# A hybrid decoder layer: the input projection of the last 1024 tokens as a stage of its own, in Strassen's seven products

## The chip, the cores and the metric

One Trainium2 chip, one NeuronCore. The metric is the device time of one execution in microseconds (us), the median of several runs; a profile gives one execution instruction by instruction. PE is TensorE's matmul, PEld its weight load, DVE is VectorE, ACT is ScalarE, POOL is GpSimd, SP is the queue that issues every DMA of this kernel.

## The reference, cut to what matters

One decoder layer is run for a prompt of 2048 tokens and for 8 sample tokens that share its weights. Each token is a row of 1024 numbers.

```python
h = rmsnorm(x, g_mix_pre)
proj = h @ w_in                       # 1024 x 4608
u_ssm, u_pool, q_mem, gates = proj[:512], proj[512:1024], proj[1024:1536], proj[1536:]   # by columns
o_ssm  = s5_branch(u_ssm)             # complex scan over time, gelu, then y * sigmoid(y @ w_glu + b)
o_pool = pool_branch(u_pool)          # trailing means over 2, 4, 8, 16 tokens, 128x128 map, scale
o_mem  = mem_attention(q_mem)         # 4 heads over 256 memory tokens
merged = sum_b sigmoid(gates_b) * (o_b @ w_branch_up[b])      # b = ssm, pool, mem
x = x + rmsnorm(merged @ w_out, g_mix_post)
x = x + rmsnorm(swiglu(rmsnorm(x, g_ffn_pre)), g_ffn_post)
```

The s5 scan and the pooling windows run along time, so a quarter of the tokens needs what the quarter before it left (`carry`, `hist`). All arithmetic is float32. A matmul of float32 quality is made of three matmuls of a faster type: both operands are split into a high and a low part (`split`: ACT copies the high part, DVE or POOL subtracts), and hi·hi, hi·lo and lo·hi are added up in PSUM.

## The kernel before

The prompt is worked on in four quarters of 512 tokens (`NQ`, `TQ`); quarter 1 carries the 8 samples too. Channels lie on the 128 partitions, tokens along the free dimension. A *block* below is one tile of 128 output channels from 1024 input channels for one quarter: 8 slices of the input, 3 matmuls each, 24 matmuls of 512 columns (`mmk`). Every weight tile is loaded (512 KB), split on ACT and DVE (on POOL for the kinds in `ON_POOL`) and used; a fixed list `_SEQ` says in which order, and `prefetch` keeps `AHEAD` = 3 of them under way.

The mixing stage (pool `mix`) does one quarter after the other:

- `ssm_project`: 4 blocks with tokens on the partitions; its result is turned by transposes in `s5_group`.
- `projections`: 4 blocks for the queries (`q_project`), 4 for the pool branch (`pool_project`), and woven among them the attention: `scores`, `transposed`, `attend`, and `pool_mix`.
- `gates`: for each of three branches 8 pairs of a gate block (`gt`, 24 matmuls) and a branch-up block (`ub`, 12 matmuls, input 512 channels); the sigmoid of the first times the second is added to `acc`. Before the branch that needs it, `glu` runs on the s5 output.
- `out_project`: 8 blocks; `residual` then needs the row norm of all of them, adds x and writes the new x to DRAM.

What isn't on the main chain of matmuls (s5 of the quarter, norms, residual of the quarter before) is written as generators in `background`, and `step` takes one piece of it between blocks; `flush` takes all that is left. A scheduler then orders the instructions of each engine by place in the program; `tc.high_priority(offset=n)` moves a piece up by n places. The main matmuls keep their order (`Tensor`).

The feed-forward input (`ffn_in`, pool `half`) already works in Strassen's form, on two quarters at once: `sums` writes the seven left operands to DRAM (`d_S`), `left` reads them back through the 4 buffers `xr` and splits them into 56 tiles `S`, `w_pair` makes the seven right operands from two weight tiles, and `product` runs each as 24 matmuls of half a quarter's width: 4 slices, 3 matmuls, 2 halves. So two blocks for two quarters take 168 matmuls of 256 (or 258) columns. `LEAD` = 700 moves the first `left` forward. A tile of a new pool waits for the tile whose memory it takes (`reuse_waits="tile"`). The last stage (pool `down`) is the feed-forward output.

At the change from mixing to feed-forward, `residual` of quarter 3 isn't in the background: it is run to its end (`run(res)`). It loads x through `xr` (`load_x`), and in program order these loads stand ahead of those of `left`.

Of the kernel before, what the change touches and what calls it, by code (L numbers as in the profile page):

```python
# [19 lines left out]
P = 128  # L20
# [14 lines left out]
SB = ((0, 1), (2, 3))  # L35
KH = KD // 2
# [9 lines left out]
AHEAD = 3  # L46
STEPS = ((1, 1, 1), (2, 1, 1), (1, 1, 1), (1, 1, 1))
# [9 lines left out]
def _weight_plan():  # L57
# [16 lines left out]
    for q in range(NQ):  # L74
# [5 lines left out]
        seq += wo + us if q + 1 < NQ else wo  # L80
    for sb in range(len(SB)):
        seq += [("f1", f) for f in range(NF)]
# [3 lines left out]
    return seq  # L86


_SEQ = _weight_plan()
_STORED = [k for k in dict.fromkeys(_SEQ) if k[0] not in ("KT", "V", "f1")]  # L90
_STORED += [(k, f) for f in range(NF) for k in ("fa", "fb")]
# [37 lines left out]
def trunk(ctx, tc, nc, I, O):  # L129
# [5 lines left out]
    BUFS = {"U": 5, "G": 2, "ops": 6, "h": 16, "br": 24, "acc": 8, "rb2": 1,  # L135
            "xr": 4, "tmp": 7, "rb": 1, "wr": 4, "wh": 4, "wl": 4, "wt": 2,
            "ev": 4, "S": 56, "f": 52, "z": 8}
    SIZE = {"tmp": 528, "ops": 512, "G": 512, "wr": 1024, "wh": 1024, "wl": 1024, "wt": 1024,
            "ev": HW_, "S": HW_, "f": HW_, "z": HW_}
    COMMON = ("xr", "tmp", "rb", "rb2", "wr", "wh", "wl")  # L140
# [6 lines left out]
    def slot(tag, dt=F32):  # L147
        n = nm(tag)
        p = base if tag in COMMON else stage[0]
        return p.tile([P, SIZE.get(tag, W520)], dt, tag=tag, name=n, bufs=BUFS[tag])  # L150

# [35 lines left out]
    mix = tc.tile_pool(name="mix", bufs=1, reuse_waits="tile")  # L187
    stage[0] = mix.__enter__()
    for tag in ("U", "G", "ops", "h", "br", "acc"):
        slot(tag)  # L190
    cv = small([P, 2, NB], "cv")
    pscale, bglu = cv[:, 0, :], cv[:, 1, :]
    ptab = small([P, NB, 4, 4], "ptab")
    hist = small([P, NB, 4, 4], "hist")
    V.memset(hist, 0.0)
    carry = [small([P, 16], "carry_re"), small([P, 16], "carry_im")]
# [11 lines left out]
    d_S = dram([len(SB), 7, KH, P, HW_], "d_S")  # L208
    d_f = dram([NQ, NF, P, HW_], "d_f")
# [42 lines left out]
    seq = _SEQ  # L252
    half = [None]
    wstate = {"emit": 0, "cur": 0, "buf": {}}
# [6 lines left out]
    def w_pair(f):  # L261
        wa, wb = w_load(("fa", f)), w_load(("fb", f))
# [14 lines left out]
    def w_emit(i):  # L277
        key = seq[i]
        if key[0] == "f1":
            wstate["buf"][i] = w_pair(key[1])  # L280
            return
# [15 lines left out]
    def prefetch():  # L297
        i = wstate["cur"]
        while wstate["emit"] < len(seq):
            pair = seq[wstate["emit"]][0] == "f1"  # L300
            if wstate["emit"] > i + (1 if pair else AHEAD) or pair and stage[0] is not half[0]:
                break
            w_emit(wstate["emit"])
            wstate["emit"] += 1
# [74 lines left out]
    def load_x(q, k, sl=None):  # L379
        t = slot("xr")  # L380
# [160 lines left out]
    r4 = small([P, 16], "r4")  # L541
# [235 lines left out]
    def s5_group(q, g, U, us, out):  # L777
# [6 lines left out]
        pu = psum2()  # L784
        for i in range(4):
            T.transpose(pu[:, i * P:(i + 1) * P], U[:, i * P:(i + 1) * P], ident)
        Ut = slot("U")
        S.activation(Ut[:, :512], pu, AF.Copy)
# [11 lines left out]
        Gr, Gi = slot("G"), slot("G")  # L800
# [47 lines left out]
        yT = slot("U")  # L848
        S.activation(yT[:, :TQ], pt, AF.Copy)
        if q == QS:  # L850
            V.tensor_copy(yT[:, TQ:W520], ysT)
# [3 lines left out]
    def s5(q, U, us, out):  # L855
        for g in range(4):
            yield from s5_group(q, g, U[g], us, out)

# [83 lines left out]
    def pool_project(q, m, h):  # L942
        n = width(q)
        w = wget("up", m)
        ps = pst(q)
        mmk(q, ps, w, h)
        pbt = slot("tmp")
        pb = pbt[:, :528].rearrange("p (s c) -> p s c", s=4)
        for p_, (o, nn) in zip(ps, blocks(q)):
# [53 lines left out]
    def q_project(q, m, h, qs):  # L1003
# [9 lines left out]
        if q == QS:  # L1013
            V.tensor_copy(qs[:, m, :], ps[-1][:, 256:264])
        return hi, lo
# [195 lines left out]

    def out_project(q, mg, z, st):
# [16 lines left out]
    def residual(q, z, st):  # L1229
# [5 lines left out]
        for k in range(KD):  # L1235
            xt = load_x(q, k)
# [10 lines left out]
        if q + 1 < NQ:  # L1247
            yield from second_scale(q)
# [21 lines left out]
    def sums(sb):  # L1270
        n = fwidth(SB[sb][0])
        rbs = [slot("rb"), slot("rb2")]
        for i, q in enumerate(SB[sb]):
            load_half(rbs[i], d_rb2, q)
        for k in range(KH):
            A = {}
            for i, q in enumerate(SB[sb]):
                for j in range(2):
                    t = slot("xr")
                    load_half(t, d_x2[:, k + j * KH], q)  # L1280
                    V.scalar_tensor_tensor(t[:, :n], t[:, :n], g_fpre[:, k + j * KH:k + j * KH + 1],
# [9 lines left out]
            for i, t in enumerate((A[0, 0], A[0, 1], s4, A[1, 1], s1, s2, s3)):  # L1291
                nc.sync.dma_start(d_S[sb, i, k, :, :n], t)
            yield

    PRODUCTS = (0, 1, 5, 4, 6, 3, 2)

    def left(sb):
        n = fwidth(SB[sb][0])
        got = {}
        for i in PRODUCTS:  # L1300
            for k in range(KH):
                raw = slot("xr")
                nc.sync.dma_start(raw[:, :n], d_S[sb, i, k, :, :n])
# [4 lines left out]

    def ffn_in(sb, got):
        n = fwidth(SB[sb][0])  # L1310
        w = n // 2
        for f_ in range(NF):
            B11, B21, T2, T1, T3, t4, B22 = wget("f1", f_)
            X, Z, Y = ([psum() for _ in range(2)] for _ in range(3))
            p1, u2, u3 = (slot("ev") for _ in range(3))
            f0, f1 = slot("tmp"), slot("tmp")

            def product(bank, i, wt, start):
                hi, lo = wt
                for u in range(2):  # L1320
                    us = slice(u * w, (u + 1) * w)
                    o = bank[u][:, :w]
                    for k in range(KH):
                        sl = slice(k * P, (k + 1) * P)
                        ah, al = got[i, k]
                        T.matmul(o, lhsT=hi[:, sl], rhs=ah[:, us], start=start and k == 0, stop=False,
                                 skip_group_check=not start)
                        T.matmul(o, lhsT=hi[:, sl], rhs=al[:, us], start=False, stop=False,
                                 skip_group_check=not start)
                        T.matmul(o, lhsT=lo[:, sl], rhs=ah[:, us], start=False, stop=k == KH - 1,  # L1330
                                 skip_group_check=not start)

            def both(fn):
                with tc.high_priority(offset=URGENT):
                    for u in range(2):
                        fn(u, slice(u * w, (u + 1) * w))

            def take(dst):
                both(lambda u, s: S.activation(dst[:, s], X[u][:, :w], AF.Copy))  # L1339

            def plus(dst, bank):
                both(lambda u, s: V.tensor_tensor(dst[:, s], dst[:, s], bank[u][:, :w], ADD))

            product(X, 0, B11, True)
            take(p1)
            product(Z, 1, B21, True)
            plus(p1, Z)
            step()
            product(X, 5, T2, False)
            take(u2)  # L1350
            product(Y, 4, T1, True)
            step()
            product(X, 6, T3, False)
            take(u3)
            plus(u3, Y)
            product(X, 3, t4, False)

            def f1_(u, s):
                S.activation(f1[:, s], X[u][:, :w], AF.Sigmoid)
# [274 lines left out]
```

## Time and profile before

| | |
|---|---|
| time, median of 3 runs | 3143.11 us (3140.39 to 3144.47) |
| the profiled execution: time / span | 3146.45 / 3144.5 us |
| mean granted TensorE clock | 0.975 |
| busy PE / DVE / ACT / POOL | 2996.9 / 1858.3 / 1214.7 / 741.6 us |
| quarters 2 and 3 of the mixing | about 915 to 1673 us |
| feed-forward input, output | about 1697 to 2598, 2602 to 3144 us |

The span is the time from the first to the last instruction; the time has a little more around it. "Busy" adds up an engine's instructions; a matmul's recorded duration overlaps that of the next, so PE is paced by when groups of a known number of matmuls end, not by its mean. A clock of 1.00 is 2.4 GHz, 0.5 is 1.2 GHz.

### The profile page before, as it was taken

What the parts mean: (1) busy time and instruction counts of PE and PEld (TensorE: products, weight loads), DVE (VectorE), ACT (ScalarE), POOL (GpSimd) and SP (SyncE); (2) the same over time, 40 slices, a digit from 0 to 9 for tenths busy, and PEclk for the clock granted to TensorE, in tenths of its full rate; (3) what the DMA queues carried; (4) which work ended last, traced back from release to release, by engine and by line L of the source; (5) the groups of instructions that cost most, each with busy time, mean ns of one, the idle gap of its engine ahead of it and who ended that gap; (6) DMA issues with size and microseconds to landing.
All of it is one profiled execution on the core that took longest, in us unless ns stands there. A gap on an engine that the chain in (4) does not pass through costs nothing.

```text
span 3144.5 us, 51655 instructions
## 1 busy us (share of the span) xinstructions
PE 2996.9 (95%) x20479; PEld 2764.9 (88%) x20479; DVE 1858.3 (59%) x3187; ACT 1214.7 (39%) x2105; POOL 741.6 (24%) x630
## 2 busy tenths in 40 slices
PE   7989998799999999999996999999999999999997
PEld 6778877689997888878885999999999998999997
DVE  7777756664538644585566855557555554445364
ACT  4532434322445333452333433335333334334343
POOL 2565244532245122440222000000000000011012
PEclk8989999899999999999997999999999999999999
DMA  6344333662334433354364732225222225445475
GB/s 210 112 161 138 120 121 116 163 218 91 127 121 149 137 102 127 120 174 133 110 219 143 233 114 76 78 77 175 81 81 81 81 84 176 153 153 170 159 253 171
DMA packets 205730, 433.02 MB, mean 138 GB/s; under 512 B 47472, under 2 KB 55216, under 8 KB 205488
## 3 DMA queue, kind: packets, MB, share of 16 engines
q1 hardware_dynamic: 205488, 429.72, 43.1%
q8 instruction: 160, 2.62, 0.4%
q14 instruction: 82, 0.67, 0.1%
HBM read 362.82 MB, written 66.49 MB: 137 GB/s over the span
## 4 chain that ended last, share of the span: by engine, by line
PE 82%; DVE 5%; DMA 5%; issue 3%; POOL 2%; ACT 2%; SPq 1%; DVEq 0%; POOLq 0%; ACTq 0%
PE pa L117 78%; PE pb L117 3%; DMA xr<-d_f 1%; DVE wl L172 1%; PE pb L120 1%; DMA xr<-in_ck 1%; DMA xr<-d_S 1%; DVE acc L1238 1%; DMA xr<-in_cv_t 0%; ACT wh L171 0%; SPq L679 0%; DMA ops<-d_ops 0%; POOL acc L1239 0%; DMA xr<-d_qs 0%; DVE G L815 0%
## 5 line engine op out<-in xcount | busy, mean ns | idle before, releaser
L117 PE MATMUL pa<-S,wh 128*128 128x258 f32 (+1 forms) x4928 | 887.4, 283 | 26.1 <-ACT S L171 20.1
L171 ACT ACTIVATE wh<-wr 128x1024 fp32r<-128x1024 f32 (+1 forms) x460 | 458.2, 996 | 1022.4 <-PE pa L117 744.1
L117 PEld LDWEIGHTS pa<-S,wh 128*128 128x128 f32 x4928 | 762.5, 190 | 29.4 <-ACT S L171 21.4
L117 PE MATMUL pa<-S,wl 128*128 128x258 f32 (+1 forms) x2464 | 693.6, 282 | 0.3 <-DVE wl L172 0.3
L117 PE MATMUL pa<-h,wh 128*128 128x512 f32 (+2 forms) x2560 | 667.2, 356 | 19.5 <-ACT tmp L1037 7.4
L172 DVE TENSOR_TENSOR wl<-wr,wh 128x1024 fp32r<-128x1024 f32 x372 | 434.2, 1169 | 393.5 <-ACT wh L171 380.8
L117 PEld LDWEIGHTS pa<-h,wh 128*128 128x128 f32 x2560 | 438.4, 192 | 86.5 <-ACT tmp L1037 7.6
L117 PE MATMUL pa<-br,wh 128*128 128x512 f32 (+2 forms) x1848 | 471.3, 351 | 15.0 <-ACT wh L171 8.8
L117 PE MATMUL pa<-f,wh 128*128 128x258 f32 (+1 forms) x2816 | 468.9, 283 | 5.9 <-DVE f L172 3.0
L117 PEld LDWEIGHTS pa<-S,wl 128*128 128x128 f32 x2464 | 465.6, 189 | 0.5 <-DVE wl L172 0.5
L117 PE MATMUL pa<-h,wl 128*128 128x512 f32 (+2 forms) x1280 | 420.7, 355 | 0.0
L117 PEld LDWEIGHTS pa<-f,wh 128*128 128x128 f32 x2816 | 400.1, 190 | 8.4 <-DVE f L172 4.3
L117 PEld LDWEIGHTS pa<-br,wh 128*128 128x128 f32 x1848 | 311.6, 190 | 62.8 <-ACT wh L171 8.8
L172 POOL TENSOR_TENSOR wl<-wr,wh 128x1024 fp32r<-128x1024 f32 (+1 forms) x88 | 214.2, 2436 | 442.2 <-ACT wh L171 392.5
L117 PE MATMUL pa<-f,wl 128*128 128x258 f32 (+1 forms) x1408 | 312.3, 283 | 4.5 <-DVE wl L172 4.5
L117 PE MATMUL pa<-br,wl 128*128 128x512 f32 (+2 forms) x924 | 295.4, 350 | 1.0 <-DVE wl L172 1.0
L117 PEld LDWEIGHTS pa<-h,wl 128*128 128x128 f32 x1280 | 231.4, 192 | 33.6
L1365 POOL TENSOR_TENSOR tmp<-tmp,ev 128x516 f32<-128x516 f32 (+1 forms) x44 | 59.9, 1362 | 841.2 <-ACT tmp L1364 820.9
L172 DVE TENSOR_TENSOR wl<-wt,wh 128x1024 fp32r<-128x1024 f32 x88 | 108.1, 1228 | 223.5 <-ACT wh L171 223.5
L117 PEld LDWEIGHTS pa<-f,wl 128*128 128x128 f32 x1408 | 229.8, 189 | 4.7 <-DVE wl L172 4.7
L117 PEld LDWEIGHTS pa<-br,wl 128*128 128x128 f32 x924 | 164.1, 190 | 24.3 <-DVE wl L172 1.4
L1339 ACT ACTIVATE ev<-pa 128x258 f32<-128x258 f32 (+1 forms) x264 | 101.0, 385 | 196.7 <-PE pa L117 166.8
(329 smaller groups left out, 3486.7 us busy)
## 6 DMA issues: line engine op xcount, KB each, us to landing
wr<-in_w_all SPq DMA_DIRECT2D x408, 512.0 KB, 3.5
ops<-d_ops SPq DMA_DIRECT2D x112, 256.0 KB, 3.6
xr<-in_x_t SPq DMA_DIRECT2D x80, 256.0 KB, 3.7
xr<-d_x SPq DMA_DIRECT2D x72, 256.0 KB, 4.1
wr<-in_w_all SPq DMA_DIRECT2D x40, 384.0 KB, 3.4
d_f<-tmp SPq DMA_DIRECT2D x44, 258.0 KB, 4.7
xr<-d_f SPq DMA_DIRECT2D x44, 258.0 KB, 3.7
d_f<-tmp SPq DMA_DIRECT2D x44, 256.0 KB, 4.3
```

What stands on the lines that cost most here:

```text
L117: self._done(self.nc.tensor.matmul(*a, **k))
L120: self._done(self.nc.tensor.transpose(*a, **k))
L171: S.activation(dst_hi, src, AF.Copy)
L172: (eng or V).tensor_tensor(dst_lo, src, f(dst_hi), SUB)
L1238: V.tensor_tensor(zk, zk, rb[:, :n], MUL)
L1339: both(lambda u, s: S.activation(dst[:, s], X[u][:, :w], AF.Copy))
L1365: G.tensor_tensor(f0[:, :n], f0[:, :n], p1[:, :n], MUL)
```

## The change

Quarters 0 and 1 stay as they are, except that the norm statistics of quarters 1 to 3 are all taken in quarter 0, and that quarter 1 has `sums_mix(1)` in its background: it writes the seven left operands of the normed x of quarters 2 and 3 to `d_h`. After quarter 1 three stages follow, each with its own pool:

- `ahead`: all 36 blocks of the input projection of quarters 2 and 3 as 18 pairs in seven products (`in_spilled`, on `seven`, which is the old body of `ffn_in`). Results, gates after their sigmoid, go to `d_p` in DRAM. In the background: s5 of quarter 2 (`s5_spilled`, its input read from `d_p`, its output written to `d_y`) and the `sums` of the first two quarters for the feed-forward.
- `late`: for quarters 2 and 3 the rest of the mixing (`mix_spilled`): `glu`, then 3 x 8 branch-up blocks whose gates are read back; during the first 8 of them (`beside`) the attention and the pool branch, from read-back projections. s5 of quarter 3 is the background of quarter 2, the residual of quarter 2 that of quarter 3. `PACE` says how many pieces per block.
- `half` and `down` as before; `f` has 50 tiles instead of 52.

The residuals of quarters 1 and 3, which end a pool, load x through `U`, not `xr`.

```diff
+MQ = (0, 1)
+PAIRS = [(("uc", 0), ("uc", 1)), (("uc", 2), ("uc", 3)), (("uq", 0), ("uq", 1)), (("uq", 2), ("uq", 3)),
+         (("up", 3), ("up", 2)), (("up", 1), ("up", 0))]
+PAIRS += [(("gt", b, j), ("gt", b, j + 1)) for b in (0, 1, 2) for j in range(0, 8, 2)]
+PACE = (1, 2, 2)
...
+    seq += [("seven", *p) for p in PAIRS]
+    for q in SB[1]:
+        seq += glu + ub(0)[:2] + [("pw",)] + ub(0)[2:] + ub(1) + ub(2) + wo
...
-    def s5_group(q, g, U, us, out):
+    def s5_group(q, g, U, us, out, tag="U", gtag="G"):
...
+        if U is None:
+            src = d_p[q % 2, SPILL["uc", g]].rearrange("(i h c) (s n) -> h s c i n", i=4, h=2, s=4)
+            for h in range(2):
+                for s in range(4):
+                    rows = slice(64 * h + 16 * s, 64 * h + 16 * s + 16)
+                    nc.sync.dma_start(Ut[rows, :512].rearrange("p (i n) -> p i n", i=4), src[h, s])
+        else:
+            pu = psum2()
+            for i in range(4):
+                T.transpose(pu[:, i * P:(i + 1) * P], U[:, i * P:(i + 1) * P], ident)
+            S.activation(Ut[:, :512], pu, AF.Copy)
...
+    def mix_spilled(q):
+        yT = []
+        for g in range(4):
+            t = slot("U")
+            nc.sync.dma_start(t[:, :TQ], d_y[q % 2, g])
+            yT.append(t)
+        KV = []
+        for src in (d_kt, d_v):
+            raw, hi, lo = slot("wr"), slot("kv", F32R), slot("kv", F32R)
+            nc.sync.dma_start(raw, src)
+            split(hi, lo, raw, G)
+            KV.append((hi, lo))
+        br = [glu(q, yT), [None] * NB, [None] * NH]
+        if q + 1 < NQ:
+            background.append(s5_spilled(q + 1, "U", "G"))
...
+        def beside(j):
+            if j < NH:
+                qt[j] = q_load(q, j)
+                pd[3 - j] = pool_project(q, 3 - j, None)
+            if 0 <= j - 1 < NH:
+                es[j - 1] = scores(q, j - 1, qt[j - 1], KV[0])
+            if 0 <= j - 2 < NH:
+                pT[j - 2] = transposed(q, j - 2, es[j - 2])
+            if 0 <= j - 4 < NH:
+                br[2][j - 4] = attend(q, j - 4, pT[j - 4], KV[1])
+                br[1][7 - j] = pool_mix(q, 7 - j, pd[7 - j], pw)
+        for b in range(3):
+            for j in range(KD):
...
+                gt = slot("gt")
+                nc.sync.dma_start(gt, d_p[q % 2, SPILL["gt", b, j]])
+                pu = psum()
+                mmk(q, [pu], wub, br[b], off=(j % 2) * NB * P)
...
+                with tc.high_priority(offset=URGENT):
+                    V.tensor_tensor(t, gt, pu, MUL)
+                if b == 0:
+                    with T:
+                        beside(j)
+                else:
+                    (V if b == 2 else G).tensor_tensor(acc[j][:, :TQ], acc[j][:, :TQ], t, ADD)
+                if b == 2:
+                    hi, lo = slot("br", F32R), slot("br", F32R)
+                    split(hi[:, :TQ], lo[:, :TQ], acc[j][:, :TQ])
+                    out.append((hi, lo))
+                step(PACE[b])
+        flush()
...
-            xt = load_x(q, k)
+            xt = load_x(q, k, tag="U" if q in (MQ[-1], NQ - 1) else "xr")
...
+    def in_spilled(got, *then):
+        for ka, kb in PAIRS:
+            out = slot("tmp")
+            fn = AF.Sigmoid if ka[0] == "gt" else AF.Copy
+            def corner(s, x):
+                S.activation(out[:, s], x, fn)
+            def end(c11, c12, c22):
+                for t, i, key in ((c11, 0, ka), (out, 1, ka), (c22, 1, kb), (c12, 0, kb)):
+                    if t is not out and fn != AF.Copy:
+                        S.activation(t[:, :TQ], t[:, :TQ], fn)
+                    nc.sync.dma_start(d_p[i, SPILL[key]], t[:, :TQ])
+            seven((ka, kb), got, TQ, corner, end)
+            if kb == ("uc", 3):
+                background.extend(then)
...
+    run(res)
+    mix.__exit__(None, None, None)
+
+    ahead = enter("ahead", {"wr": 3, "wt": 2, "ev": 3, "ops": 4, "S": 56}, {"ev": TQ, "S": TQ})
+    with tc.high_priority(offset=LEAD):
+        prefetch()
+        got = left(d_h, TQ)
+    background.append(second_scale(1))
+    in_spilled(got, s5_spilled(2, "xr", "xr"), sums_ffn(0))
+    flush()
+    ahead.__exit__(None, None, None)
+
+    late = enter("late", {"wr": 4, "U": 5, "G": 2, "ops": 6, "gt": 6, "kv": 4, "br": 24, "acc": 8})
+    for q in SB[1]:
+        mg = mix_spilled(q)
...
     run(res)
-    mix.__exit__(None, None, None)
...
+    late.__exit__(None, None, None)
+    half = enter("half", {"wr": 4, "wt": 2, "ev": 4, "S": 56}, {"ev": HW_, "S": HW_})
```

## Rows read from the trace of the kernel before

**Rows 1.** The page: busy time by engine; the chain that ended last, by engine

```profile
PE 2996.9 (95%) x20479; PEld 2764.9 (88%) x20479; DVE 1858.3 (59%) x3187; ACT 1214.7 (39%) x2105; POOL 741.6 (24%) x630
...
PE 82%; DVE 5%; DMA 5%; issue 3%; POOL 2%; ACT 2%; SPq 1%; DVEq 0%; POOLq 0%; ACTq 0%
```

**Rows 2.** Stretches: length; PE, PEld, DVE, ACT, POOL busy; clock; DMA share; GB/s

```profile
100.00:200.00 100.00, 85.63 (x406) 70.01 (x405) 82.96 (x219) 46.22 (x90) 64.59 (x119) 0.92 0.40 131
...
934.00:1026.00 92.00, 84.54 (x421) 68.24 (x420) 69.56 (x129) 47.09 (x107) 48.15 (x39) 0.98 0.44 147
...
1673.00:1697.00 24.00, 3.93 (x18) 3.61 (x18) 18.96 (x29) 7.74 (x13) 13.33 (x8) 0.54 0.48 149
1697.00:1744.00 47.00, 37.35 (x249) 34.92 (x248) 38.89 (x72) 26.20 (x47) 1.67 (x1) 0.84 0.74 230
...
1744.00:2161.00 417.00, 417.00 (x3487) 417.00 (x3488) 254.13 (x421) 158.68 (x283) 29.78 (x21) 1.00 0.39 115
```

**Rows 3.** Timeline of ACT: evictions of `out_project` (L1223) and of `ssm_project` (L770)

```profile
934.53 2.89 ACT L770 ACTIVATE U<-pa 128x128 f32<-128x128 f32 x16 [2.37 <-PE pa L117]
...
1282.85 0.58 ACT L1223 ACTIVATE tmp<-pa 128x512 f32<-128x512 f32 x1
...
1293.97 0.58 ACT L1223 ACTIVATE tmp<-pa 128x512 f32<-128x512 f32 x1
...
1313.38 2.87 ACT L770 ACTIVATE U<-pa 128x128 f32<-128x128 f32 x16 [2.38 <-PE pa L117]
```

**Rows 4.** Timeline of ACT in `ffn_in`: the same eviction of two successive tiles

```profile
2561.42 0.39 ACT L1339 ACTIVATE ev<-pa 128x256 f32<-128x256 f32 x1 [0.85 <-PE pa L117]
...
2581.31 0.39 ACT L1339 ACTIVATE ev<-pa 128x256 f32<-128x256 f32 x1 [0.85 <-PE pa L117]
```

**Rows 5.** Chain of waits, one piece of s5: 16 small matmuls

```profile
1048.85 1.78 PE pb L117 x16
```

**Rows 6.** Timelines of ACT, DVE, POOL, SP where mixing gives way to feed-forward

```profile
1672.88 0.60 ACT L1223 ACTIVATE tmp<-pa 128x512 f32<-128x512 f32 x1 [4.38 <-PE pa L117]
...
1681.16 11.31 DVE L1238 TENSOR_TENSOR acc<-acc,rb 128x512 f32<-128x512 f32 x8 [2.27 <-ACT rb L372]
...
1681.93 13.33 POOL L1239 TENSOR_TENSOR acc<-acc,xr 128x512 f32<-128x512 f32 x8 [27.90 <-DVE acc L1238]
...
1690.28 0.33 SPq L1303 DMA_DIRECT2D xr<-d_S  x1
...
1695.83 1.14 ACT L171 ACTIVATE S<-xr 128x516 fp32r<-128x516 f32 x2
```

**Rows 7.** The page: DMA issues, KB each, median us from issue to landing

```profile
d_f<-tmp SPq DMA_DIRECT2D x44, 256.0 KB, 4.3
xr<-d_f SPq DMA_DIRECT2D x44, 256.0 KB, 4.2
```

**Rows 8.** Groups of POOL, 934 to 1313 us: busy us, mean ns

```profile
L172 POOL TENSOR_TENSOR wl<-wr,wh 128x1024 fp32r<-128x1024 f32 x21 | 51.8, 2466 | 96.6 <-ACT wh L171 96.6
...
L172 POOL TENSOR_TENSOR br<-U,br 128x512 fp32r<-128x512 f32 x4 | 5.7, 1429 | 68.9 <-ACT br L171 68.8
```

**Rows 9.** Groups of DVE, 934 to 1313 us: busy us, mean ns

```profile
L172 DVE TENSOR_TENSOR wl<-wr,wh 128x1024 fp32r<-128x1024 f32 x40 | 50.5, 1262 | 54.1 <-ACT wh L171 49.9 <-PE pb L117 3.8
L1226 DVE TENSOR_TENSOR tmp<-tmp,tmp 128x512 f32<-128x512 f32 x7 | 18.0, 2571 | 10.2 <-ACT tmp L1223 10.2
L814 DVE TENSOR_TENSOR_SCAN G<-r,carry_re,G 128x128 f32<-128x128 f32 x16 | 12.4, 832 | 1.4 <-POOL G L807 1.4
...
L1238 DVE TENSOR_TENSOR acc<-acc,rb 128x520 f32<-128x520 f32 x8 | 10.6, 1378 | 0.6 <-ACT rb L372 0.6
...
L815 DVE TENSOR_TENSOR_SCAN G<-r,carry_im,G 128x128 f32<-128x128 f32 x16 | 6.4, 459 | 0.0
...
L820 DVE TENSOR_TENSOR tmp<-G,ops 128x512 f32<-128x512 f32 x4 | 2.7, 684 | 0.1
```

More of the change, by code (lines that the diff above doesn't have):

```diff
@@ L85, in _weight_plan @@
     seq += fo
[L86 to L91, printed above, removed]
+    ends.append(len(seq))
+    return seq, ends
+_SEQ, _ENDS = _weight_plan()
+_STORED = []
+for _k in _SEQ:
+    _STORED += [x for x in (_k[1:] if _k[0] == "seven" else [_k]) if x[0] not in ("KT", "V") and x not in _STORED]
 _WIDX = {k: i for i, k in enumerate(_STORED)}
@@ L150, in slot, with enter, keep @@
         return p.tile([P, SIZE.get(tag, W520)], dt, tag=tag, name=n, bufs=BUFS[tag])
+    def enter(name, bufs, sizes=()):
+        for tag in list(BUFS):
+            if tag not in COMMON:
+                del BUFS[tag]
+        BUFS.update(bufs)
+        SIZE.update(sizes)
+        guard = tc.tile_pool(name=name, bufs=1, reuse_waits="tile")
+        stage[0] = guard.__enter__()
+        for tag in bufs:
+            slot(tag)
+        wstate["end"] = ends.pop(0)
+        return guard
+    def keep(shape, tag):
+        return base.tile(shape, F32, tag=tag, name=nm(tag), bufs=1)
     def small(shape, tag, bufs=1, dt=F32):
@@ L298, in prefetch @@
         i = wstate["cur"]
-        while wstate["emit"] < len(seq):
-            pair = seq[wstate["emit"]][0] == "f1"
-            if wstate["emit"] > i + (1 if pair else AHEAD) or pair and stage[0] is not half[0]:
+        while wstate["emit"] < wstate["end"]:
+            if wstate["emit"] > i + (1 if seq[wstate["emit"]][0] == "seven" else AHEAD):
                 break
@@ L1371, in load_f @@
+            seven((("fa", f_), ("fb", f_)), got, n, corner, end)
     def load_f(q, n):
@@ L1472, in trunk @@
     background.append(s5_first(U, yT))
-    for q in range(NQ):
+    for q in MQ:
         br = [None] * 3
@@ L1480, in trunk @@
                 br[0] = glu(q, yT)
-                background.append(norm_stats(q + 1) if q + 1 < NQ else sums(0))
+                if q == 0:
+                    background.extend(norm_stats(j) for j in range(1, NQ))
+                else:
+                    background.append(sums_mix(1))
             if b == 2 and q == QS:
@@ L1512, in trunk @@
             prefetch()
-            got = left(sb)
+            got = left(d_S[sb], fwidth(SB[sb][0]))
         if sb + 1 < len(SB):
             background.append(second_scale(NQ - 1))
-            background.append(sums(sb + 1))
+            background.append(sums_ffn(sb + 1))
         ffn_in(sb, got)
         flush()
-    second.__exit__(None, None, None)
-    down = tc.tile_pool(name="down", bufs=1, reuse_waits="tile")
-    stage[0] = down.__enter__()
-    slot("z")
+    half.__exit__(None, None, None)
+    down = enter("down", {"wr": 4, "z": 8, "f": 50})
     for q in range(NQ):
```

251 lines of the change are left out of this document (146 added, 105 removed).

## The prediction

> **What bounds the kernel now.** I read the page first: PE is busy 95% of the span, and 82% of the chain that ended last is PE [rows 1]. So a saving of matmul time counts in full where PE is back to back, and the question is where it isn't. The view of stretches shows where: PE is full in the feed-forward input, idle 7.5 of 92 us while a quarter's projections and attention run, and far from full for 71 us where mixing gives way to feed-forward [rows 2]. Then I read the pace of PE off evictions that wait for it: two `out_project` blocks end 11.12 us apart, so a block of 24 matmuls of 512 columns takes 5.56 us, 0.2315 us each; `ssm_project`'s four blocks take 1313.38 - 1293.97 = 19.4 us; and one `ffn_in` tile of 168 matmuls of 256 columns takes 2581.31 - 2561.42 = 19.9 us, 0.1184 each [rows 3, 4]. Half the columns cost 0.511 of the time, so halving the width gives away little of the eighth that seven products save.
>
> **The saving on PE.** Removed for two quarters: 2 x (19.4 + 32 x 5.56) = 394.6 us. Added: 18 pairs x 19.9 = 358.2 us. Also removed are 32 transposes of the s5 input, at 1.78/16 = 0.11 us each [rows 5]: 3.5 us. Together -39.9 us. This half is well founded: the new stage is the same code as the stage that rows 4 are from. Everything below is about what the cut costs.
>
> **Hand-over 1, quarter 1 to `ahead`.** Before, `ssm_project` of quarter 2 followed at once and the residual of quarter 1 hid in the background. Now that residual is run to its end, as quarter 3's is today. What that does today: the last block ends at 1672.9, the norm chain takes 8.3 us, then eight steps of DVE and POOL 1.67 us apart, and the first `left` load is issued only at 1690.3, because the residual's x loads hold the `xr` buffers; the first split of an S tile is at 1695.8, and in the 71 us to 1744 PE gets through 249 feed-forward matmuls of 0.12 us plus small ones, about 31 us [rows 2, 6]. So today's hand-over costs 40 us, part of it at the low clock (0.54 and 0.84). The new one is better placed: x comes through `U`, so `left` may load and split during `out_project`, into memory that `h` has left. Of the right operands, t34 lies where two `U` buffers lay, so it waits for the residual, 8 to 24 us after the last block; the four products before it (96 matmuls, 11.4 us) don't. The last S tiles take the memory of `acc`, which is free when the last new x is in DRAM: 8 + 13 + about 2 + 4.3 us [rows 6, 7], then a load (4.2) and a split: some 33 us, when an unhindered first pair would be over at 19.9. The first pair then ends near 36: I take +17 us; bounds 10 and the 40 of today.
>
> **`ahead` itself.** DVE is busy 254 of 417 us in today's stage with PE full [rows 2]. Per 19.9 us pair it keeps four differences, the low halves and six additions, and loses the four swiglu products; it gains s5 of quarter 2 (57 us, below). That is some 75%, spread in 48 pieces. PE has no other cover to lose here: +2 us, bounds 0 and 10. The extra DMA (1 MB written per 20 us, and DMA share 0.39 there now) hides.
>
> **Hand-over 2, `ahead` to `late`.** `glu` needs four `yT` in `U`; two of these lie where the last pair's `ev` tiles lie. These must be added up, go through a sigmoid, be stored (4.3 us) and only then can `yT` be loaded (4.2 us) and split, the low half on POOL (1.43 us) [rows 7, 8]. Nothing else stands on PE's main chain. About 1.5 + 4.3 + 4.2 + 2 = 12 us; bounds 8 (what is on POOL goes early) and 20 (POOL does the four K/V and GLU splits of 2.47 us first).
>
> **The mixing that is left.** Here cover is gone. A branch-up block had a gate block of 5.56 us beside it; now its 12 matmuls (2.78 us) stand alone, while DVE keeps almost all its work. Per quarter PE has 48 + 288 + 36 matmuls of 512 (86 us), 48 of 256 (5.7), 48 transposes and small ones (7): 99 us up to `out_project`; in quarter 2 also s5 of quarter 3, 160 matmuls of 0.11: 117 us. DVE in quarter 2: 12 low halves at 1.26, 84 operations of 512 columns at 0.69 (GLU 8, queries 4, pool 8, attention 20, pool map 4, gate products 24, sums and splits of the third branch 16), 5 of small ones: 78 us; s5: 32 scans (18.8 us), 48 operations at 0.68, 6 of others: 57 us [rows 9]. 135 us of DVE against 117 of PE: DVE becomes the bound of quarter 2's mixing. At 100% busy that costs 18 us; at the 83% that DVE reached in the start, where it is the bound today [rows 2], 163 - 117 = 46. I take 27, nearer the lower end, since the start is one serial set-up and here four groups and a main chain interleave, and some query and pool work can run in hand-over 2. Quarter 3 has no s5, but the residual of quarter 2 (11.3 us as in rows 6, plus 8) falls into its first 8 blocks: DVE there 45 + 19 = 64 against PE's 55: +12 with friction. Then 2 x 2 us because the first branch-up block now waits for `glu`'s last split. Together 43. What goes away: a quarter today takes 1313.38 - 934.53 = 378.9 us for 19.4 + 177.9 + 564 x 0.2315 + 5.7 + about 31 of small matmuls = 364.6 us [rows 3], so 14 us per quarter, 28 for two, are lost in the stretches removed. Net +15 us; bounds -5 (18 + 5 - 28) and +45 (46 + 23 + 4 - 28).
>
> **Hand-over 3, `late` to feed-forward.** Today's 40 us. Now `left` needn't wait for `xr`; but both `wt` buffers lie under `U`, which the residual holds until about 22 us. Two products (5.7 us) run at once, then PE waits to about 25, starts at the low clock, and finishes the tile after 14 to 18 us: 25 + 16 - 20 = 21. Gain -18 us; bounds -25 and 0 (nothing gained).
>
> **Hidden.** `sums_mix(1)` in quarter 1's last gates: the same work (`sums`) runs in quarter 3's last gates today. The two norms more in quarter 0 lie under its last gates. The 6 fewer `f` tiles still leave room ahead. s5's 8 small loads per group stand on SP among loads that have their time. 0, bounds 0 and 4.
>
> **The sum.** -39.9 + 17 + 2 + 12 + 15 - 18 = -11.9 us against the profiled execution's own 3146.45: 3134.5. That execution is 3.3 us above the median of the runs shown, so 3131 us.
>
> **A rule against it.** `L1226` takes 2571 ns in the stretch where POOL makes the low halves of `wo` (2466 ns each), although an addition of that size takes 684 [rows 8, 9]; `L1238`, alternating with POOL, takes 1378. So VectorE and GpSimd hold each other up here. The Trainium skill, "SBUF — State Buffer", "Who interferes with whom", says why: the pair of ports that both share is locked for a whole instruction, and a VectorE operation with two SBUF inputs stands still while a GpSimd operation reads SBUF. By that rule, the trace agrees, the late mixing is the worst place for it, since POOL's work there (GLU and K/V splits, pooling sums, attention scaling) isn't made less.
>
> **The rivals.**
> - *VectorE with POOL in its way bounds the late mixing (slower).* Price: the excess seen in one quarter today, 7 x 1.9 + 8 x 0.7 + 16 x 0.37 = 25 us [rows 9], half of it beside `out_project` where DVE is idle. The scans' 6 are counted already; if the other 19 all fall into quarter 2's mixing and a third of them into quarter 3's, the late loss is 27 + 19 + 12 + 6 + 4 = 68, net +40: -39.9 + 17 + 2 + 12 + 40 - 18 = +13, 3156 us. It decides from a net late loss of 27 us on. For it: 135 against 117. Against: POOL is busy only 48 of 92 us in today's densest stretch. Chance 0.18.
> - *Every hand-over costs what today's costs (slower).* If `left` isn't early, hand-over 1 costs 40, hand-over 3 gains nothing: -39.9 + 40 + 2 + 14 + 15 + 0 = +31, 3174 us. For it: the order is a scheduler's. Against: `xr` is what held `left`, and it is free now. Chance 0.09.
> - *It evens out.* Hand-over 1 at 24 and late +20: -39.9 + 24 + 2 + 12 + 20 - 18 = 0, 3143 us. Chance 0.18.
> - *The cuts hide better than I think.* 10, 0, 8, -5, -25 with the saving: -52, 3091 us; half-way 3110. Chance 0.13.
> - That the seven products don't save: their pace would have to miss 21.9 us per pair; rows 4 say 19.9. Under 0.02, inside the others.
>
> **The numbers.** Forecast 3131 us, chance 0.42, own range 3112 to 3137. 0.2% is 6.3 us, about what a measurement of this kernel can tell from no change. Faster: 0.42 + 0.13 = 0.55; same 0.18; slower 0.27. The range 3095 to 3172 leaves out the extreme of the good case and the worst of the second rival.
>
> **What would show it.** `ahead`: evictions of one pair 19.9 us apart, PE full. Hand-over 1: from `out_project`'s end to the end of the first pair about 37 us. Hand-over 2: some 12 us without PE. Late quarter 2: DVE over 90% busy and about 145 us up to `out_project`; quarter 3 about 113. Hand-over 3: S tiles split before the last block ends. I am wrong if PE is full in the late mixing, or if `left` starts only after the residual, or if a pair takes over 20.5 us.

## The result, and the profile after

The changed kernel takes 3233.99 us (median of 4 runs, 3229.54 to 3240.11) against 3141.75 us for the kernel before beside it: a ratio of 1.0296, 95% interval 1.0275 to 1.0318, some 92 us slower. The prediction said 3131 us, at most 3172, and was wrong. The profiled execution has a span of 3233.5 us at a mean granted clock of 0.957 (before: 3144.5 at 0.975).

The view of stretches of the changed kernel, one row per stage: hand-over 1, `ahead`, quarter 2, quarter 3, hand-over 3. It answers to [rows 2].

```profile
core 0: us, PE busy (x) PEld busy (x) DVE busy (x) ACT busy (x) POOL busy (x), PEclk, DMA share, GB/s
912.00:985.00 73.00, 41.88 (x276) 39.28 (x276) 59.02 (x104) 34.20 (x63) 13.54 (x8) 0.72 0.64 210
985.00:1337.00 352.00, 351.18 (x2967) 350.98 (x2966) 212.58 (x360) 136.37 (x245) 11.06 (x8) 1.00 0.48 156
1336.20:1575.20 239.00, 180.05 (x820) 143.87 (x820) 146.30 (x230) 86.54 (x146) 95.20 (x61) 0.89 0.50 163
1575.20:1760.20 185.00, 157.14 (x676) 125.47 (x676) 115.17 (x175) 71.27 (x132) 76.58 (x53) 0.92 0.38 117
1760.20:1830.00 69.80, 39.05 (x251) 36.47 (x252) 56.44 (x99) 33.35 (x56) 14.06 (x9) 0.73 0.66 212
```

Where the new stage runs, it runs as forecast: PE is busy 351.18 of 352 us at full clock, 2967 matmuls, 0.1184 us each, the pace of [rows 4]. Everything lost is at the edges of `ahead` and in what follows. DVE, the rival for the bound, is busy 146 of 239 us in quarter 2, 61% as a mean over the quarter.

The stages by profile, in us. `ahead` runs from the last eviction of quarter 1's `out_project` to the last matmul on S; quarters 2 and 3 each end at their `out_project`'s last eviction; the feed-forward input ends at its last matmul.

| kernel | ahead | quarter 2 | quarter 3 | ff input | output | span |
|---|---|---|---|---|---|---|
| before | 757.6 for all three | | | 924.3 | 546.2 | 3144.5 |
| forecast | 395 | 202.5 | 157.5 | 906 | 546 | 3123 |
| after | 422.8 | 239.0 | 185.0 | 925.7 | 547.6 | 3233.5 |
| e1_residual1_in_ahead | 408.9 | 232.2 | 184.2 | 925.2 | 548.1 | 3213.0 |
| e2_residual3_in_half | 421.9 | 236.2 | 186.7 | 914.1 | 546.9 | 3221.0 |
| e3_s5_both_in_ahead | 446.6 | 175.1 | 178.3 | 925.4 | 546.9 | 3184.6 |
| e4_kv_after_glu | 423.9 | 234.6 | 185.1 | 928.6 | 545.3 | 3232.8 |
| e7_pace_222 | 422.7 | 221.6 | 186.0 | 926.9 | 546.6 | 3220.0 |
| e5_z_apart | 421.9 | 231.9 | 180.9 | 925.7 | 547.5 | 3226.5 |
| e8_z_apart_residual2_later | 422.5 | 229.8 | 178.8 | 924.8 | 547.5 | 3220.6 |
| e11_wr_common | 421.4 | 230.5 | 183.4 | 923.8 | 543.1 | 3217.0 |
| e9_all | 437.7 | 181.5 | 163.6 | 910.0 | 548.1 | 3156.9 |
| e10_all_wr_common | 433.4 | 174.0 | 170.0 | 908.7 | 543.5 | 3141.0 |
| e13_residual2_spilled | 433.5 | 175.1 | 171.8 | 906.1 | 543.6 | 3142.1 |
| e12_attention_spread | 433.7 | 176.5 | 184.9 | 907.7 | 545.9 | 3161.8 |
| b1_before_residual3_in_half | | | | 909.6 | 541.8 | 3123.0 |

The forecast's row is the prediction's terms put together by stage (395 = 358 + 18 of s5's matmuls + 17 + 2; 202.5 = 12 + 117 + 27 + 2 + 44.5; 157.5 = 99 + 12 + 2 + 44.5); by stage they add up to 9 us less than by differences. The misses: `ahead` 28, quarter 2 36, quarter 3 27, feed-forward input 19. A stage that an edit doesn't touch still moves by some us (quarter 2 is between 229.8 and 239.0 in the kernels that leave its work alone): each program is scheduled anew, and executions of one kernel differ too (3229.54 to 3240.11 us for the changed one). So an edit is read from its own stage, and a difference below some 9 us there isn't shown by one profile.

### The profile page after: what moved, and what is told of

It reads as the page before. It is cut to its first block, busy times and chain, and to the rows that moved or that the text cites. A ratio compares the mean times of both kernels' runs of the same rounds, so it can differ in the third digit from the quotient of the medians.

```text
span 3233.5 us, 55015 instructions
## 1 busy us (share of the span) xinstructions
PE 2983.0 (92%) x21743; PEld 2817.2 (87%) x21743; DVE 1963.9 (61%) x3411; ACT 1250.2 (39%) x2201; POOL 709.1 (22%) x614
## 5 line engine op out<-in xcount | busy, mean ns | idle before, releaser
L133 PE MATMUL pa<-S,wh 128*128 128x256 f32 (+1 forms) x6944 | 1254.4, 284 | 51.5 <-ACT wh L203 40.0
L133 PEld LDWEIGHTS pa<-S,wh 128*128 128x128 f32 x6944 | 1076.5, 190 | 56.6 <-ACT wh L203 40.6
L133 PE MATMUL pa<-S,wl 128*128 128x256 f32 (+1 forms) x3472 | 979.0, 283 | 3.5 <-DVE wl L204 3.5
L203 ACT ACTIVATE wh<-wr 128x1024 fp32r<-128x1024 f32 (+2 forms) x420 | 407.9, 972 | 821.1 <-PE pa L133 636.9
L133 PEld LDWEIGHTS pa<-S,wl 128*128 128x128 f32 x3472 | 657.6, 190 | 4.3 <-DVE wl L204 4.3
L133 PE MATMUL pa<-h,wh 128*128 128x256 f32 (+2 forms) x1536 | 340.8, 328 | 12.6 <-ACT tmp L1091 7.4
L133 PEld LDWEIGHTS pa<-h,wh 128*128 128x128 f32 x1536 | 245.5, 194 | 36.1 <-ACT tmp L1091 7.6
L1457 ACT ACTIVATE ev<-pa 128x256 f32<-128x256 f32 (+1 forms) x372 | 142.1, 385 | 273.3 <-PE pa L133 238.2
L133 PE MATMUL pa<-h,wl 128*128 128x512 f32 (+2 forms) x768 | 216.9, 327 | 0.0
L1460 DVE TENSOR_TENSOR ev<-ev,pa 128x256 f32<-128x256 f32 (+1 forms) x372 | 154.2, 418 | 67.7 <-PE pa L133 43.8
```

Source lines behind the costliest of these rows:

```text
L133: self._done(self.nc.tensor.matmul(*a, **k))
L203: S.activation(dst_hi, src, AF.Copy)
L1457: both(lambda s, u: S.activation(dst[:, s], X[u][:, :w], AF.Copy))
L1460: both(lambda s, u: V.tensor_tensor(dst[:, s], dst[:, s], bank[u][:, :w], ADD))
```

## The experiments

Changes of the time below are differences of ratios to the kernel before, times 3142 us; each has some 8 us of uncertainty.

**The hand-overs: `e1_residual1_in_ahead`, `e2_residual3_in_half`, `b1_before_residual3_in_half`.** The new residual is the old one with its tiles read back:

```diff
+            if q in SPQ:                      # in out_project: 1, or 3
+                nc.sync.dma_start(d_z[q, m, :, :n], z[m][:, :n])
...
+            zt = slot("xr")                   # in residual_spilled
+            in_turn(nc.sync.dma_start(zt[:, :n], d_z[q, k, :, :n]))
...
-    run(res)
     mix.__exit__(None, None, None)
...
-    background.append(second_scale(1))
+    background.append(residual_spilled(1, st))
```

> Quarter 1's out_project writes its eight raw tiles to DRAM, and its residual reads them back through xr as background of ahead; nothing of the residual stands between the two stages. Theory A (the new stage starts as one piece behind the last user of the old one, which is the residual's last Square at 935.2, with the first S split at 935.75): the first S split and weight load move to within 5 us of the last out_project eviction at 913, some 20 us earlier, and the time falls by 15 to 25 us from 3234, to 3209 to 3219. Rival B (what the hand-over loses is the start itself: weight load, differences, splits and matmuls at the low clock): the splits may come earlier but the first pair doesn't end earlier by more than 8 us, time 3226 or more. Rival C (the residual's loads and stores crowd the loads of left): no gain or a loss.

> The same for quarter 3: its residual becomes the first background of the feed-forward input. Theory A: the first S split, at 1781.6 right behind the last Square at 1781.0, moves to within 5 us of the last out_project eviction at 1759; the time falls by 15 to 25 us from 3234, which is the 18 us that the prediction had put down for this hand-over. Rival B (start-up itself): 8 us or less.

> The kernel before, with only the edit of the experiment on quarter 3's residual: raw tiles to DRAM, residual as first background of the feed-forward input. If what that edit gives is a matter of the hand-over and not of the change under study, it gives 12 to 18 us here too: 3141.5 - 15, 3124 to 3130. If the hand-over before was shorter for another reason (xr held by the residual): 0 to 8 us.

Ratios 1.0239 [1.0222, 1.0256], 1.0251 [1.0233, 1.027] and 0.9951 [0.9934, 0.9967]: 18, 14 and 15 us faster than the kernels they are made from; by stage 14, 12 and 15 us. The timeline of the changed kernel at hand-over 1, ACT then SP:

```profile
912.90 0.49 ACT L1337 ACTIVATE acc<-pa,gv 128x264 f32<-128x264 f32 x1
...
935.21 0.64 ACT L1355 ACTIVATE tmp<-acc 128x520 f32<-128x520 f32 x1 [1.07 <-POOL acc L1352]
935.75 2.18 ACT L203 ACTIVATE S<-xr 128x512 fp32r<-128x512 f32 x4
...
930.11 5.41 SPq L1353 DMA_DIRECT2D d_x<-acc  x4
935.57 1.39 SPq L287 DMA_DIRECT2D wr<-in_w_all  x3
```

The four S tiles come from `xr` buffers whose loads had been issued at 853.7 to 856.0; they lay there for 80 us. The first split follows the residual's last Square (the ACT instruction that squares a new x for the next norm) at once, the first weight load the residual's last store. The same of the first experiment:

```profile
913.90 0.49 ACT L1340 ACTIVATE acc<-pa,gv 128x264 f32<-128x264 f32 x1
914.27 2.20 ACT L203 ACTIVATE S<-xr 128x512 fp32r<-128x512 f32 x4
...
875.36 39.38 SPq L1344 DMA_DIRECT2D d_z<-acc  x8
914.84 1.35 SPq L288 DMA_DIRECT2D wr<-in_w_all  x3
```

The splits follow whatever is last on ACT of the old pool, now an eviction, and start while SP is still issuing the store of that tile, so they don't wait for that tile's memory: in the order of ACT and SP the new pool's instructions stand behind the old pool's. Theory A holds in its effect, and the "one piece" is an order, not a release of memory. At hand-over 3 it is the same: the view of PE's waits from 1750 to 1850, first of the changed kernel, then of the second experiment.

```profile
PE pa L133 <- ACT wh L203: 20.1, 1, 20.1
```

```profile
PE pa L133 <- ACT wh L203: 6.8, 2, 6.6
```

Counted in the traces, the first 168 matmuls on S, one pair's worth, end 63.1 us after the last eviction of `out_project` in the changed kernel and 41.2 us after it in the first experiment, where the prediction had 36. At hand-over 3 they end after 62.1 us, and after 40.5 in the second experiment, where the prediction had 25 + 16 = 41; in the kernel before, after 60.4. So rival B (the start itself) fails, and the forecast lengths come out nearly, once the residual is out of the way. Of the 22 us by which the start moves, 14 and 12 are left at the end of the stage; where the rest goes is not shown.

And the kernel before had this loss too, which is [rows 6]; there the edit alone gives 3128.81 us against 3144.16 beside it, faster than both kernels of this study.

**s5 in the late mixing: `e3_s5_both_in_ahead`, `e7_pace_222`.** The first takes s5 of quarter 3 out of quarter 2's mixing, the second issues it earlier there.

```diff
-            background.append(s5_spilled(q + 1, "U", "G"))
...
-    in_spilled(got, s5_spilled(2, "xr", "xr"), sums_ffn(0))
+    in_spilled(got, s5_spilled(2, "xr", "xr"), s5_spilled(3, "xr", "xr"), sums_ffn(0))
```

```diff
-PACE = (1, 2, 2)
+PACE = (2, 2, 2)
```

> s5 of quarter 3 leaves quarter 2's mixing and runs in ahead behind s5 of quarter 2, with two background pieces instead of one at two of a pair's three places. Theory D (s5's serial chain of some 38 us per group holds up ACT and PE in order, above all in out_project, where six PSUM tiles wait while ACT waits 17.9 us for s5's last matmuls): late quarter 2, 238 us from 1335.5 to 1574, falls to 180 to 195, ahead grows by its 18 us of matmuls and up to 10 more, and quarter 3 no longer waits for s5's last store: time 3234 - 20 to - 40, 3194 to 3214. Rival E (the cost only moves: PE in ahead waits for DVE, which goes from 212 to about 270 of 352 us): within 8 us of 3234.

> The first eight branch-up blocks take two background pieces each instead of one, so s5 of quarter 3 is issued some four blocks earlier, with the same work on every engine. Theory D (s5's chain ends inside out_project and holds ACT there): s5's last matmuls come before out_project, the 17 us wait in out_project goes, time 3234 - 10 to - 20, 3214 to 3224. Rival J (VectorE's throughput bounds quarter 2's mixing): the order changes and the sum doesn't; within 6 us of 3234, since what s5 does earlier the attention does later. Rival K (the chain's own length, 38 us for each of four groups one behind the other, sets the end): also no gain.

Ratios 1.0142 [1.0126, 1.0157] and 1.0239 [1.0224, 1.0254]: 48 us and 18 us faster. With s5 gone, quarter 2 falls by 64 us, `ahead` grows by 24, 18 of which are s5's matmuls, and quarter 3 gains 7. Earlier s5, with the same work on every engine, takes 17 us off quarter 2, or 8 if one counts from the lowest of the kernels that leave its work alone: so not DVE's throughput over the quarter alone (rival J), and not only the chain's own length (rival K). How the other 30 of the 48 us divide isn't shown, since moving s5 takes its DVE work along with its order. The waits of PE in quarter 2 of the changed kernel (us in total, times, longest):

```profile
PE pb L133 <- DVE G L863: 17.3, 2, 12.5
PE pa L133 <- ACT wh L203: 14.9, 1, 14.9
PE pa L133 <- ACT br L203: 5.8, 4, 4.3
PE pb L136 <- ACT tmp L1098: 5.7, 1, 5.7
```

of the one with earlier s5, where the last group still ends inside `out_project`, but the wait for it falls from 12.5 to 1.3 us, while another one before s5's matmuls, 7.3 us at 1443, comes up:

```profile
PE pb L133 <- issue: 7.3, 1, 7.3
...
PE pb L133 <- DVE G L864: 1.3, 1, 1.3
```

and of the one with s5 in `ahead`, where such waits are gone:

```profile
PE pa L133 <- ACT wh L203: 13.4, 1, 13.4
PE pb L136 <- ACT tmp L1098: 4.2, 1, 4.2
```

The timeline of the changed kernel inside quarter 2's `out_project` shows how the 12.5 us come about (POOL, DVE, ACT, PE):

```profile
1544.29 2.34 POOL L204 TENSOR_TENSOR kv<-wr,kv 128x1024 fp32r<-128x1024 f32 x1
1546.59 1.26 POOL L842 TENSOR_TENSOR G<-G,tmp 128x512 f32<-128x512 f32 x1
...
1547.88 2.59 DVE L849 TENSOR_TENSOR_SCAN G<-r,carry_re,G 128x128 f32<-128x128 f32 x4 [4.30 <-POOL G L842]
...
1541.19 1.06 ACT L203 ACTIVATE kv<-wr 128x1024 fp32r<-128x1024 f32 x1
1560.15 0.60 ACT L903 ACTIVATE tmp<-pb 128x512 f32<-128x512 f32 x1 [17.91 <-PE pb L133]
1560.65 0.59 ACT L1336 ACTIVATE tmp<-pa 128x512 f32<-128x512 f32 x1
...
1555.47 1.39 PE L133 MATMUL pb<-ops,G 128*128 128x128 f32 x4 [12.48 <-DVE G L863]
```

The last group's scans wait for POOL, which had K/V and weight splits in front; PE waits for the scans; ACT stands 17.91 us on the gelu that needs PE's result, and behind it in ACT's order stand the evictions of `out_project`, six blocks of them. Three queues in order hand one late group to the main chain.

That DVE's 61% is a mean matters: in two stretches of the same quarter it is near 90%, while PE idles 5 to 7 of 20 us (the columns are those of the view by stage). So its throughput isn't excluded as a limit there.

```profile
1396.00:1416.00 20.00, 13.17 (x64) 10.42 (x63) 17.70 (x40) 11.65 (x30) 10.64 (x11) 0.83 0.30 94
...
1496.00:1516.00 20.00, 14.91 (x68) 11.35 (x66) 18.23 (x24) 4.35 (x5) 10.04 (x5) 0.97 0.41 140
```

**Quarter 2's residual in quarter 3: `e5_z_apart`, `e8_z_apart_residual2_later`.**

```diff
-            z.append(slot("acc"))
+            z.append(slot("z" if q > QS else "acc"))   # 8 tiles z; gt 4 instead of 6
```

```diff
-                step(PACE[b])
+                step((PACE if q < NQ - 1 else (0, 2, 2))[b])   # with z apart
```

> In late, out_project's results get eight tiles z of their own instead of the eight acc (gt goes from 6 buffers to 4 to make room). Theory F (quarter 3's first gate products write acc tiles that still hold the old quarter's result until residual has stored it: the product at 1620.7 stands behind eight multiplies of 10.1 us, and PE waits 12.1 us for it): the first gate product no longer waits, quarter 3 falls from 185 us to 165 to 175, time 3214 to 3224. Rival G (those products wait for DVE, POOL and loads of gates anyway): within 6 us of 3234, or a loss from the fewer gt buffers.

> As with the z tiles apart (3227), but quarter 3's first eight branch-up blocks take no background piece; the residual of quarter 2 comes in the second eight. Theory L (with z apart the wait only moved, since eight multiplies of the residual, 9.2 us in a row on DVE, stood ahead of the attention's scores: PE waited 13.1 us for the softmax): the waits in the first eight blocks lose 12 to 18 us, quarter 3 falls from 181 us to 165 to 170, time 3210 to 3216. Rival G (throughput of DVE over the quarter): 3223 or more.

Ratios 1.0274 [1.0258, 1.0289] and 1.0252 [1.0237, 1.0267]; by their own stage 4 and 6 us, less than expected; the first doesn't differ from the changed kernel by more than its uncertainty. The changed kernel:

```profile
1610.75 10.06 DVE L1351 TENSOR_TENSOR acc<-acc,rb 128x512 f32<-128x512 f32 x8
1620.74 0.68 DVE L1311 TENSOR_TENSOR acc<-gt,pa 128x512 f32<-128x512 f32 x1
1621.46 1.65 PE L133 MATMUL pa<-kv,br 128*128 128x256 f32 x6 [12.10 <-DVE acc L1311]
```

The first gate product stands behind eight multiplies of the residual. With z apart it comes at 1599.77, and this wait is gone; but the longest waits of PE in quarter 3 are then, in the two experiments in turn:

```profile
PE pb L136 <- ACT tmp L1098: 13.1, 1, 13.1
```

```profile
PE pb L133 <- DVE rb L1357: 8.1, 1, 8.1
```

A softmax behind the same eight multiplies, and, with the residual later, the row sums of the residual's own norm (`second_scale`). The wait moved twice. That the first product waited (theory F) is true and was worth little; theory L explains the second wait, not the size.

**Where the new stages' weights lie: `e4_kv_after_glu`, `e11_wr_common`.** The first moves the loading of K and V behind `glu`. The second takes `wr` out of the pools, as it was before the change (three buffers instead of the four then):

```diff
-    BUFS = {"xr": 4, "tmp": 7, "rb": 1, "rb2": 1, "wh": 4, "wl": 4}
+    BUFS = {"wr": 3, "xr": 4, "tmp": 7, "rb": 1, "rb2": 1, "wh": 4, "wl": 4}
```

> In late, K and V are loaded and split behind glu instead of ahead of it. Theory H (at the change from ahead to late, PE's 14.9 us without work end with the split of glu's first weight tile, whose load is issued behind K and V on SP and whose split stands behind theirs on ACT: 1340.2, 1340.7, 1341.1 and 1347.4, 1348.7, 1350.0): the wait falls to 9 to 11 us, the low half of K and V leaves POOL free for glu's input, and the same happens in quarter 3; time 3234 - 4 to - 10, 3224 to 3230. Rival I (the wait is for the last stores to DRAM and the loads of glu's input): no change in the wait.

> The changed kernel with only the weight buffers put outside the pools, three for the whole program. Theory M: glu's first weights no longer stand behind the pool's change, so PE's 14.9 us between ahead and late fall to about 9, and the first right operands of ahead and of the feed-forward input are split while the residual runs, but their S tiles still stand behind it; -5 in each place at most, time 3234 - 8 to - 18, 3216 to 3226. Rival: 3230 to 3240, since the S tiles set those starts and three buffers are fewer than four.

The changed kernel at hand-over 2 (SP, ACT, PE):

```profile
1340.18 0.42 SPq L1275 DMA_DIRECT2D wr<-d_kt  x1
1340.65 0.43 SPq L1275 DMA_DIRECT2D wr<-d_v  x1
1341.12 1.21 SPq L319 DMA_DIRECT2D wr<-in_w_all  x2
...
1347.43 1.06 ACT L203 ACTIVATE kv<-wr 128x1024 fp32r<-128x1024 f32 x1 [2.51 <-DMA wr<-d_kt]
1348.71 1.06 ACT L203 ACTIVATE kv<-wr 128x1024 fp32r<-128x1024 f32 x1 [0.23 <-DMA wr<-d_v]
1349.99 1.06 ACT L203 ACTIVATE wh<-wr 128x1024 fp32r<-128x1024 f32 x1 [0.22 <-DMA wr<-in_w_all]
...
1351.10 3.69 PE L133 MATMUL pa<-br,wh 128*128 128x512 f32 x8 [14.92 <-ACT wh L203]
```

With K and V later the wait is 10.2 us, but the ratio, 1.0278 [1.0263, 1.0293], doesn't differ from the changed kernel's by more than its uncertainty: inconclusive. With `wr` common the wait is for `glu`'s input, 8.7 us, and the ratio is 1.0247 [1.0231, 1.0264], 15 us faster, 8.5 of them by stage in quarter 2, where 6 are this wait. At hand-overs 1 and 3 the common weights give 1 and 2 us only; at hand-over 3 PE then waits for S instead of `wh`, 18.2 us in all.

**All together: `e9_all`, `e10_all_wr_common`, `e13_residual2_spilled`, `e12_attention_spread`.** The edits above in one kernel (with `second_scale(2)` moved into the feed-forward input); that with three common `wr` (and `gt` 5 instead of 4); that with quarter 2's residual read back too, and its memory given to `br` and `gt`; and that with the attention spread:

```diff
-                if b == 0:
+                if b < 2:
                     with T:
-                        beside(j)
+                        beside(8 * b + j)      # scores, transposes, values of head m at 2m+4, 2m+6, 2m+8
```

> The edits so far in one kernel: residuals of quarters 1 and 3 as background of the next stage, s5 of both quarters in ahead, K and V behind glu, z apart, quarter 2's residual in the second eight blocks of quarter 3, and the norm that belongs to it moved out of out_project into the feed-forward input. If the causes are separate places, their gains add up: 3234 - 19 - 15 - 49 - 11 - 2 to - 6 gives 3134 to 3138, just under the kernel before (3141 to 3144). If they are one shared limit (DVE's throughput, or PE's clock that stays low whatever waits), the sum is less: 3150 or more.

> As the kernel with all edits, and the weight buffers wr are three for the whole program, outside the stages' pools, as four of them were in the kernel before; then the first weights of a stage can be loaded and split while the old one ends. Theory M (part of each hand-over is that the first weight loads stand behind the old pool's last store: 914.8 in the experiment on quarter 1, 1341 for glu): each of three hand-overs loses 4 to 8 us less, 12 to 24 in all, 3112 to 3126. Rival: three buffers instead of four cost as much elsewhere, 3130 to 3140.

> As the kernel with all edits and common weight buffers, but quarter 2's residual also goes through DRAM and xr, so z needs no tiles of its own; the memory goes to br (32 instead of 24) and gt (6 instead of 5). The order of the work is the same. Theory N (a part of the late mixing's loss is that the eight tiles of glu's output stay in the br ring until the eighth branch-up block, and the attention's and pool branch's results wait for them): quarters 2 and 3 lose 3 to 8 us each, 3130 to 3140. Rival: buffers aren't what is waited for; 3142 to 3150.

> The same, and the attention is spread over the first sixteen branch-up blocks (a new head every two blocks, four blocks from scores to the weighted values) instead of the first eight. Theory O (what the late mixing loses is latency: a head's chain scores, softmax, transposes, values is stepped once per 2.8 us block, where before a step had 8 us and more, and PE in its order waits for it): the waits for softmax and splits in the first eight blocks go, the clock stays up, quarters 2 and 3 lose 8 to 15 us each against the same kernel without the spreading, 3115 to 3130. Rival P (DVE's and POOL's throughput): the work is the same, within 6 us of the kernel without the spreading.

Ratios 1.0048 [1.0031, 1.0066], 1.0009 [0.9998, 1.002], 1.0007 [0.9998, 1.0016] and 1.0074 [1.0058, 1.0091]. The first misses the sum of the single ratios by 22 us and lies where one shared limit was expected, at 3150 or more. By stage it nearly adds up: 3233.5 - 14 - 12 - 47 - 6 = 3154.5 against a span of 3156.9. That speaks for separate places and for drift in stages that an edit doesn't touch, but with a drift of up to 9 us in a stage it doesn't decide. Common `wr` gives 12 us more. Then the change is level with the kernel before; against the kernel before with its own residual moved behind hand-over 3 (0.9951) it is still 18 us slower. More buffers (theory N) give nothing. Spreading the attention (theory O) makes it slower, nearly all of it in quarter 3: 171.8 to 184.9 us there, 175.1 to 176.5 in quarter 2. One wait for the softmax in quarter 3 is

```profile
PE pb L136 <- ACT tmp L1099: 16.8, 1, 16.8
```

That softmax had its row maxima at 1597.85. On ACT it stands behind six Squares of quarter 2's residual, which wait, by way of POOL's sums, for tiles read back from DRAM; the last Square and the softmax are

```profile
1625.63 0.63 ACT L1384 ACTIVATE tmp<-xr 128x512 f32<-128x512 f32 x1 [3.23 <-POOL xr L1381]
1626.17 0.46 ACT L1092 ACTIVATE tmp<-pa,mx 128x256 f32<-128x256 f32 x1
```

The residual had been put into the second eight blocks, and the spread attention now lies there too. So in quarter 3 this run shows a collision and is no clean test of theory O; in quarter 2, where no residual runs, the spreading changes nothing beyond drift.

In the first of the two that are level, with all edits and common `wr`, quarters 2 and 3 look like this, with two stretches of quarter 3 below:

```profile
1344.80:1518.80 174.00, 151.88 (x660) 120.57 (x661) 99.37 (x130) 75.64 (x134) 77.38 (x54) 0.95 0.47 148
1518.80:1688.80 170.00, 151.52 (x645) 117.17 (x643) 118.63 (x160) 71.55 (x129) 72.83 (x51) 0.94 0.46 146
...
1604.00:1624.00 20.00, 20.00 (x87) 16.09 (x86) 20.00 (x16) 6.33 (x9) 18.17 (x11) 1.00 0.73 236
1624.00:1644.00 20.00, 16.65 (x57) 10.67 (x56) 19.61 (x23) 7.15 (x10) 10.19 (x5) 0.85 0.63 198
```

PE idles 22 and 18 us, on many small waits, and is busy some 8 us longer than the 143.5 that the matmuls were counted at; DVE is 57 and 70% busy, but full from 1604 to 1644. What sets these small waits stays open: not buffers in the `br` ring, and in quarter 2 not the attention's density; DVE's throughput isn't excluded where it is full.

## Why the prediction was wrong

**The saving on PE, -39.9 us, and `ahead` itself, +2:** right. The pace is the forecast one, and no DVE or DMA work slowed it (DMA share 0.48).

**Hand-over 1, +17, and hand-over 3, -18:** this step failed. It let `left` load and split during `out_project`, "into memory that `h` has left". The loads did come early (853.7), the splits and the weight loads didn't: they stand behind the residual's last instruction in ACT's and SP's order. `ahead` cost 28 us more than forecast, and the feed-forward input gained nothing on [rows 6]: PE's longest wait there was 20.1 us. So +17 became about 45 and -18 became +1; with the residual out of the way the first 168 matmuls end 41.2 and 40.5 us after the block, against the forecast 36 and 41. I saw the order in [rows 6], the first split right behind the residual's end, and read it as a full `xr`. The second rival had the mechanism here, 40 and 0 for the two; it was given 0.09. A move I overlooked, `wr` from common memory into the pools, is no part of this step: undoing it gives 15 us, but 1 and 2 at these two places.

**Hand-over 2, +12:** 14.9 us; near. What remains with common `wr`, 8.7 us, is the wait for `glu`'s input that the step had priced at 12; the other 6 it had put at nothing ("nothing else stands on PE's main chain"): `glu`'s weights, which stood behind K and V.

**The late mixing, net +15:** this step failed too, and is the largest miss, 36 + 27 us less 3 at hand-over 2. I priced it as DVE's throughput, 135 us of work against 117 of PE's. The 135 was near (146 measured, `out_project` included). But the 83% that made DVE a bound came from a row in which PE is busier than DVE, 85.63 against 82.96 of 100 us [rows 2], and over the quarter DVE reached 61%: what the runs show instead is order. s5's four groups run one after the other, the last three 36 to 38 us each from first matmul to store, and the last ended inside `out_project`, holding ACT and PE by their order; moving s5 gives 48 us, issuing it earlier 18 (30 of the 48 are not divided between order and DVE's work). In quarter 3 the residual's eight multiplies stand in one row before the first gate products; I had counted their time, not what queues behind them. And where PE waits it then works at a lower clock: mean 0.89 in quarter 2, so that matmuls counted at 161.5 us kept PE busy for 180.

**The rival of VectorE with POOL in its way:** its price of 3156 came about nowhere. The eight multiplies beside POOL's sums do take 10.06/8 = 1.26 us each against 0.684 for a multiply of that size in [rows 9], which agrees with the Trainium skill, "SBUF — State Buffer", "Who interferes with whom". But a DVE that is 61% busy over the quarter isn't bound by that as a whole; one place where the stretched instructions cost is shown, the first gate product of quarter 3 behind them. No run takes POOL's work away, so the rest of this rival is untested.

**Hidden, 0:** held for `sums_mix(1)`: quarter 1's `out_project` ends at 913.4, against 916.5 before.

## What to carry to other kernels

When a stage is cut in two, price first what runs to its end at the cut: here, on ACT and SP, the next stage's first instructions stood behind the old stage's last, so work off the main chain (a residual, a recurrence) belongs behind the cut, with its operands in DRAM or in memory that both stages share. Cover that is removed isn't replaced by free throughput: compare what each in-order queue holds when a late piece arrives, not busy times alone. And read a single edit from its own stage, since the others drift by several us.

## What the runs showed of the hardware

A wait cost PE twice. In the 73 us of hand-over 1 it was busy 41.88 us at a mean granted clock of 0.72 (of 2.4 GHz), where its 276 matmuls at `ahead`'s pace would take about 33 (an estimate, 276 x 0.1184); in the 70 us of hand-over 3 the clock was 0.73. In `ahead`, with PE busy 351.18 of 352 us, it was 1.00. I had priced waits by their length alone, except in one place.
